# Another order of eight heads, sweeps half a step ahead, and one bfloat16 matmul for a sum, in a bidirectional linear-attention block

## The chip, the cores and the metric

The kernel runs on one core of a Trainium2 chip. The metric is the device time of one execution in microseconds (us); lower is better. Five engines work side by side, each through its own queue in order: TensorE (PE; its weight loads are shown apart, as PEld), VectorE (DVE), ScalarE (ACT), GpSimd (POOL) and SyncE (SP, which issues most transfers).

## What is computed

One transformer block on 2048 tokens of width 1024, with 256 context tokens and a conditioning vector `c`. Cut to what matters:

```python
mod_x = silu(c) @ w_mod + b_mod                    # six vectors: sh1 sc1 g1 sh2 sc2 g2
hx = rmsnorm(x) * (1 + sc1) + sh1                  # and hc from the context, with its own vectors
p = hx @ w_in                                      # queries, keys or gates, values of 8 heads
# heads 0-3, HGRN2: f = lb + (1 - lb) * sigmoid(z), decay f per key element, both directions
# heads 4-7, retention: rope on q and k, one decay per head, both directions
mixed = norm and gate of (forward scan + backward scan)    # scans start from context states
x = x + g1 * (mixed @ w_out)
gate, up = split(rmsnorm2(x) @ w_up); gate = conv3(gate)
x = x + g2 * ((silu(gate) * up) @ w_down)
return rmsnorm(x) * final_g
```

## The kernel before

Every large product is made of float16 pairs: a float32 value is a rounded float16 and a float16 rest, and `mm3` (lines 88 to 90) adds three of the four products. Blocks are combined so that seven block products stand for eight (`unit`), whose inputs, called features (`hx` for the tokens, `hc` for the context), are sums and differences of blocks that `first_blocks` makes once and keeps in DRAM (`hxd`).

The program has these stages. `setup` loads the first slices of `w_mod` and the last 512 tokens. `heads` forms the modulation and the features of the last token group, and then walks 32 steps: eight heads with four token groups (512 tokens) each, the last group first. In step (h, i) `step` runs the backward scan of head h on group 3 - i (`hg_sweep1` for HGRN2, `ret_sweep1` for retention), and the forward scan of the head before it on group i (`hg_sweep2`, `ret_sweep2`), which leaves the scaled output to a second part (`hg_sweep2b`, `ret_sweep2b`: multiply, transpose on PE, store). The projection of the next group or head is a generator that `weave` puts between the pieces of the step. In the first steps of the first head the features of the context and of groups 1 and 0 are still made, also as pieces (`with_blocks`). An HGRN2 scan works through seven levels; at each DVE multiplies the tiles `K` and `Q` by products of gates, and PE multiplies pieces of them into `sc` or `sf`. A retention scan has one product of scores (`rsc`), one multiply with a table (`rA`) and four small state updates. During the heads, `tick` also prepares the next head's weights (`w_z`, `w_q`, `w_vg`: `wx<-raw` rows), and in the retention heads the later slices of the modulation: `mod_later` multiplies rows of `w_mod` into `macc` on DVE. `ret_consts` makes the tables of retention; it is called at the third head.

After the heads come the output product (`opp`), the up product of the feed-forward part (`ffn_up`: 11 pairs of column blocks, with the weights of each of the two halves of a pair prepared one unit ahead in `up_weights`, so 22 times), and the down product (`ffn_down`). `up_weights` squares the raw weights on ACT, sums the squares over partitions on PE (`allsum`), and takes a power of two from the sum on DVE (`pow2`).

The order on each engine is decided at build time by a scheduler that reorders the instructions of the program text; each engine then runs its list in order. The line that sums over partitions before:

```python
self.nc.tensor.matmul(o, self.onesq, cols[:, i:i + 1], start=i == 0, stop=i == n - 1, ...)   # float32, twice
```

Of the kernel before, what the change touches and what calls it, by code (L numbers as in the profile page):

```python
# [43 lines left out]
SEQUENCE = 0, 1, 5, 6, 4, 3, 2  # L44

# [9 lines left out]
class Kern:  # L55
# [57 lines left out]

    def allmax(self, col, tag="tu"):
# [10 lines left out]
    def setup(self):  # L125
# [42 lines left out]
        self.W0, self.items0 = self.head_weights(0)  # L168
# [22 lines left out]
        self.smalls = s2, s1  # L191

# [32 lines left out]
    def mod_rows(self, rows, nr, j4):  # L225
# [12 lines left out]
        bm = view(self.sv, V_BM + 4 * j4, [[1, 4], [0, nr]])  # L238
        nc.vector.tensor_tensor(o, ps[:, :, :nr], bm, ALU.add)

    def mod_loads(self):
# [4 lines left out]
        for j4, places in ((2, ("hx",) * 4), (3, ("hx",) * 4), (0, KEPT[:4]), (1, ("FG", "KTt", "ou0", "ou1"))):  # L246
# [8 lines left out]
            if j4 in (3, 1):  # L255
                self.items0[0 if j4 == 3 else 4][0]()
# [14 lines left out]
    def mod_later(self, j4):  # L271
# [5 lines left out]
        def item(k0):  # L277
            def load():

                st[k0] = w = [self.slot_tile([P, 512], F32, "q", "wm") for _ in range(2)]  # L280
                for kk in range(2):
                    nc.sync.dma_start(w[kk], wsrc[:, k0 + kk, 512 * j4:512 * j4 + 512])

            def comp():
                if k0 == 0:
                    st["acc"] = self.slot_tile([P, 512], F32, "FG", "macc")
# [9 lines left out]
                if k0 + 2 == KT:  # L296
                    self.mod_rows(acc, 1, j4)
# [209 lines left out]
    def unit(self, mm, shape, banks, temps, evac, lin=(None, None), first=False):  # L507
# [5 lines left out]
        if first:  # L513
# [28 lines left out]
            add(tb, tb, u, ALU.add)  # L542
# [123 lines left out]
    def head_weights(self, h):  # L666
# [11 lines left out]
        for nm, tag, cols in want:  # L678
            raws, st = [], {}

            def load(cols=cols, raws=raws, tag="ou2" if h == 0 and nm == "q" else "wr"):
# [4 lines left out]
            def start(nm=nm, tag=tag, raws=raws, st=st):  # L686
# [7 lines left out]
                s, neg, dq = self.scales(self.allsum(ssq), self.dqx[:, 0:1] if h else None, "dq" + nm)  # L694
# [23 lines left out]
    def decay_gates(self, FG, X, h, n, W, first=False):  # L718
# [6 lines left out]
        yield from self.head_unit(*self.fm(w, X, n // 2), evac, first=first)  # L725
# [59 lines left out]
    def hg_proj(self, pool, h, g, W, pr, cur, first=False):  # L785
# [3 lines left out]
        yield from self.decay_gates(FG, X, h, G, W, first)  # L789
# [20 lines left out]
        yield from self.head_unit(*self.tm(w, X, H), evac, (dq, None), first)  # L810
# [125 lines left out]
    def hg_sweep2b(self, pool, h, g, st):  # L936
# [4 lines left out]
        m = r["qf"] if h < NH - 1 else pool.tile([P, G], F32, tag="Kl", bufs=KL, name="m")  # L941
# [3 lines left out]
    def weave(self, main, filler, n_main, n_fill):  # L945

        done = 0
# [8 lines left out]
    def step(self, h, i, W, cur, prev, pr):  # L956
# [3 lines left out]
        slot = i if h % 2 == 0 else NG - 1 - i  # L960
        hg, hgp = h < NH, h - 1 < NH
        if h < 2 * NH:
# [3 lines left out]
        if prev is not None:  # L966
# [880 lines left out]
```

## Time and profile before

| what | value |
|---|---|
| runs | 2703.32 us median of 3 (2699.55 to 2703.4) |
| the profiled execution's own time | 2701.94 us |
| its span, first to last instruction | 2699.5 us |
| busy on PE, DVE, ACT, POOL | 2544.2, 1847.7, 1344.8, 785.0 us |
| mean granted clock of PE | 0.973 of full speed |

Busy time is the union of an engine's instructions; the span less PE's busy time, 155.3 us, is what PE stood idle. A granted clock below 1 in a stretch means that part of it ran at the lower of two levels (1.2 instead of 2.4 GHz).

### The profile page before, as it was taken

The page shows a single profiled execution, that of the slowest core. Times are in us where ns is not written, and L with a number is a line of the kernel's source. Part 1 is how long each engine was busy: PE and PEld are TensorE (multiplying, and loading weights), DVE is VectorE, ACT ScalarE, POOL GpSimd, SP SyncE. Part 2 cuts the span into 40 slices and gives each one's busy share as a digit, 9 for nine tenths or more (in the row PEclk, how much of TensorE's full clock was granted, in tenths as well). Part 3 has the DMA queues.
Part 4 walks back from the last instruction along what each step waited for, and adds up shares of the span by engine and source line. Part 5 has one row for each costly group of instructions (what it writes and reads, how often), then busy time and mean ns, then how long its engine had stood idle before and what let it go on. Part 6 is the DMA issues. An engine that isn't in the chain of part 4 may idle for free.

```text
span 2699.5 us, 56351 instructions
## 1 busy us (share of the span) xinstructions
PE 2544.2 (94%) x22829; PEld 1680.0 (62%) x22829; DVE 1847.7 (68%) x3585; ACT 1344.8 (50%) x2902; POOL 785.0 (29%) x905
## 2 busy tenths in 40 slices
PE   5798999999999999998999999999999999999998
PEld 2578888888889889886454444444444444444443
DVE  4898677776767686666466788888787777323553
ACT  5776456564555444445455566565555555311120
POOL 3733112111223232221344344343443342000102
PEclk7899999999999999998999999999999999999999
DMA  8224234243337575755521232333322325635552
GB/s 297 104 87 158 96 111 146 88 138 119 121 127 257 197 246 178 239 195 180 196 98 47 94 110 101 107 105 110 117 101 103 118 88 197 254 129 187 203 194 95
DMA packets 213621, 393.98 MB, mean 146 GB/s; under 512 B 15599, under 2 KB 97747, under 8 KB 208752
## 3 DMA queue, kind: packets, MB, share of 16 engines
q1 hardware_dynamic: 203808, 373.42, 40.1%
q10 hardware_dynamic: 9248, 16.79, 1.9%
q8 instruction: 178, 2.92, 0.4%
q14 instruction: 83, 0.68, 0.1%
q0 software_dynamic: 304, 0.17, 0.0%
HBM read 298.57 MB, written 91.75 MB: 145 GB/s over the span
## 4 chain that ended last, share of the span: by engine, by line
PE 71%; DVE 15%; ACT 4%; issue 4%; DMA 3%; POOL 2%; SPq 0%; DVEq 0%; ACTq 0%; POOLq 0%
PE pa L88 8%; PE pa L89 8%; PE pa L90 8%; PE pd L89 5%; PE pd L90 5%; PE pd L88 5%; PE pc L88 4%; PE pc L89 4%; PE pc L90 4%; PE pb L88 2%; PE pb L90 2%; PE pb L89 2%; PE opp L89 2%; PE opp L88 2%; PE opp L90 2%
## 5 line engine op out<-in xcount | busy, mean ns | idle before, releaser
L88 PE MATMUL pa<-feat,w 128*128 128x512 f16 x704 | 267.9, 381 | 12.2 <-ACT ta L549 8.1
L89 PE MATMUL pa<-feat,w 128*128 128x512 f16 x704 | 268.1, 381 | 0.0
L90 PE MATMUL pa<-feat,w 128*128 128x512 f16 x704 | 264.9, 381 | 0.0
L89 PE MATMUL pd<-wd,actl 128*128 128x512 f16 x616 | 233.3, 379 | 0.0
L90 PE MATMUL pd<-wd,actl 128*128 128x512 f16 x616 | 233.3, 379 | 0.0
L88 PE MATMUL pd<-wd,actl 128*128 128x512 f16 x616 | 232.7, 379 | 0.0
L89 PEld LDWEIGHTS <-w 128*128 128x128 f16 x1232 | 120.8, 98 | 155.4 <-issue 15.6
L90 PEld LDWEIGHTS <-w 128*128 128x128 f16 x1232 | 121.4, 99 | 145.1 <-issue 1.4
L88 PEld LDWEIGHTS <-w 128*128 128x128 f16 x1232 | 121.7, 99 | 141.6 <-issue 2.4
L89 PEld LDWEIGHTS <-hx 128*128 128x128 f16 x1824 | 183.0, 100 | 8.5 <-issue 6.3
L90 PEld LDWEIGHTS <-hx 128*128 128x128 f16 x1824 | 182.6, 100 | 3.4 <-issue 2.6
L88 PEld LDWEIGHTS <-hx 128*128 128x128 f16 x1824 | 182.9, 100 | 2.2
L1598 DVE SCALAR_TENSOR_TENSOR st<-act,modT,st 128x512 f16<-128x512 f32 x154 | 144.3, 966 | 32.3 <-ACT st L1597 32.3
L1597 ACT ACTIVATE st<-act,modT 128x512 f16<-128x512 f32 x154 | 107.2, 718 | 83.9 <-DVE act L1587 30.2
L88 PE MATMUL pa<-w_vg,hx 128*128 128x128 f16 x800 | 144.7, 222 | 0.2
L89 PE MATMUL pa<-w_vg,hx 128*128 128x128 f16 x800 | 144.5, 222 | 0.0
L90 PE MATMUL pa<-w_vg,hx 128*128 128x128 f16 x800 | 144.4, 222 | 0.0
L88 PE MATMUL pc<-feat,w 128*128 128x512 f16 x352 | 133.5, 379 | 1.3 <-ACT feat L1372 1.2
L88 PE MATMUL pa<-hx,w_z 128*128 128x256 f16 x464 | 127.6, 275 | 7.5 <-DVE rV L591 4.1
L90 PE MATMUL pc<-feat,w 128*128 128x512 f16 x352 | 133.6, 380 | 0.0
L89 PE MATMUL pc<-feat,w 128*128 128x512 f16 x352 | 133.6, 380 | 0.0
L89 PE MATMUL pa<-hx,w_z 128*128 128x256 f16 x464 | 127.3, 274 | 0.0
(551 smaller groups left out, 7557.6 us busy)
## 6 DMA issues: line engine op xcount, KB each, us to landing
hx<-hxd SPq DMA_DIRECT2D x212, 512.0 KB, 4.7
actd<-st SPq DMA_DIRECT2D x154, 256.0 KB, 2.0
actl<-actd SPq DMA_DIRECT2D x28, 1024.0 KB, 5.0
wur<-in_w_up_dram SPq DMA_DIRECT2D x44, 512.0 KB, 3.9
raw<-in_w_in_dram SPq DMA_DIRECT2D x36, 512.0 KB, 4.6
wm<-in_w_mod_dram SPq DMA_DIRECT2D x64, 256.0 KB, 4.1
hxd<-hx SPq DMA_DIRECT2D x28, 512.0 KB, 3.4
wdb<-in_w_down_dram SPq DMA_DIRECT2D x44, 256.0 KB, 3.9
```

What stands on the lines that cost most here:

```text
L88: mm(ps, lhs(0), rhs(0), start=start, stop=False, skip_group_check=True)
L89: mm(ps, lhs(0), rhs(1), start=False, stop=False, skip_group_check=True)
L90: mm(ps, lhs(1), rhs(0), start=False, stop=stop, skip_group_check=True)
L1597: nc.scalar.activation(p[:, 0], v, AF.Copy, scale=s)
L1598: nc.vector.scalar_tensor_tensor(p[:, 1], v, s, p[:, 0], ALU.mult, ALU.subtract)
```

## The change

The heads are taken in the order `ORDER = 4, 0, 1, 2, 3, 5, 6, 7`: the first retention head, the four HGRN2 heads, the other three retention heads. Positions are now called `p`, heads `h`. The features of the context and of groups 1 and 0 are made beside that retention head, with another spacing of pieces in `with_blocks`. `ret_consts` moves to `setup`, with its loads on ACT's queue, and `lower_bounds` from before the first head into its second step.

In `step` the forward scan of the previous head runs half a step ahead: group 0 and, from the middle on, group 1 in step 0, group 2 from the middle of step 1, group 3 from the middle of step 2. Steps of a retention head start with two pieces of the projection (`lead`). `mod_later` makes slices 4 to 9 beside heads 5 and 6 (before: 4 to 11 beside heads 4, 5 and 6); slices 10 and 11, and the broadcast of `g2` from them, move into the first blocks of the down product (`gates_later`). `up_weights` calls `allsum16`: DVE adds the two columns into a bfloat16 one, and PE sums it with one bfloat16 matmul.

```diff
+ORDER = 4, 0, 1, 2, 3, 5, 6, 7
...
+    def allsum16(self, cols, tag):
+        both = self.wp.tile([P, 1], BF16, tag="both", bufs=2, name="both")
+        self.nc.vector.tensor_tensor(both, cols[:, 0:1], cols[:, 1:2], ALU.add)
+        o = self.ps(tag, [P, 1], "allsum")
+        self.nc.tensor.matmul(o, view(self.onesb, 0, [[0, P]]), both, start=True, stop=True, skip_group_check=True)
+        return o
...
-        self.W0, self.items0 = self.head_weights(0)
+        self.ret_loads()
+        self.W0, self.items0 = self.head_weights(ORDER[0], True)
...
+        self.ret_consts()
...
     def with_blocks(self, proj, blocks):
-        for j in range(18):
+        for j in range(14):
             next(proj)
-            if j in (5, 6, 7, 8, 9) or j > 11:
+            if 0 < j < 6 or j > 7:
                 next(blocks, None)
...
-        if prev is not None:
-            (self.hg_sweep2 if hgp else self.ret_sweep2)(pool, (h - 1) % NH, i, prev)
+        if prev is not None and (last or i == 0):
+            sweep2(pool, hp % NH, i, prev)
...
-        if prev is not None:
-            (self.hg_sweep2b if hgp else self.ret_sweep2b)(pool, (h - 1) % NH, i, prev)
+        if prev is not None and (last or i == 0):
+            sweep2b(pool, hp % NH, i, prev, not hg)
+        ahead = prev is not None and not last and i + 1 < NG
+        if ahead:
+            sweep2(pool, hp % NH, i + 1, prev)
         yield from main
...
+        if ahead:
+            sweep2b(pool, hp % NH, i + 1, prev, not hg)
...
-        first = self.hg_proj(pool, 0, NG - 1, W, pr, cur, True)
+        first = self.ret_proj(pool, ORDER[0] % NH, NG - 1, W, pr, cur, True)
...
-                        mods = [it for c in ((4, 5, 6), (7, 8, 9), (10, 11))[h - NH] for it in self.mod_later(c)]
+                        mods = [it for c in ((4, 5, 6), (7, 8, 9))[ORDER[p] - 5] for it in self.mod_later(c)]
...
-            if s == 4 * 2:
-                self.ret_consts()
+                self.lower_bounds()
...
-        s, neg, dq = self.scales(self.allsum(ssq, "sc"), self.dqx[:, 1:2], ("dqz", "dqvg")[ty])
+        s, neg, dq = self.scales(self.allsum16(ssq, "sc"), self.dqx[:, 1:2], ("dqz", "dqvg")[ty])
...
+    def gates_later(self):
+        for j4 in (10, 11):
+            ahead = None
+            for load, comp in self.mod_later(j4, ("wr", "ou0"), True):
+                load()
+                yield
+                if ahead:
+                    ahead()
+                    yield
+                ahead = comp
+            ahead()
+            yield
+        dg = self.slot_tile([P, 2, P], F32, "xs", "diag")
+        self.broadcast_cols(lambda j: dg[:, j % 2], self.gb, 40)
+        yield
...
                 self.work(1)
+                if n < 3:
+                    next(late, None)
```

What the scheduler makes of it is shown at three places. The first is DVE's list in step 1 of the third HGRN2 head, ahead of the first multiply of `Q` (`Q<-Q,FG`, level 1). `KTt` and `Sb` rows are the backward state of the step before; `Sf`, `ou<-ou,o` and `ou<-ou,gate` are the forward scan of the previous head. Before:

```order
L888 SCALAR_TENSOR_TENSOR Sb<-KTt,T_7262,ub 128x128
L102 TENSOR_SCALAR p2i<-p2t 128x1
L907 SCALAR_TENSOR_TENSOR ou<-Sf,T_4400,ou 128x128
L932 TENSOR_TENSOR ou<-ou,o_8044 128x512
L103 TENSOR_SCALAR p2s<-p2i 128x1
L663 TENSOR_TENSOR dq<-p2i,dqx 128x1
L907 SCALAR_TENSOR_TENSOR ou<-ou,T_4400 128x128
L933 TENSOR_TENSOR ou<-ou,gate 128x512
L658 TENSOR_SCALAR neg<-p2s 128x1
L907 SCALAR_TENSOR_TENSOR ou<-ou,T_4400 128x128
L853 TENSOR_TENSOR Q<-Q,FG 128x2x256
```

The same place now, on to the multiply of level 2:

```order
L903 SCALAR_TENSOR_TENSOR Sb<-KTt,T_9050,ub 128x128
L104 TENSOR_SCALAR p2i<-p2t 128x1
L105 TENSOR_SCALAR p2s<-p2i 128x1
L678 TENSOR_TENSOR dq<-p2i,dqx 128x1
L673 TENSOR_SCALAR neg<-p2s 128x1
L868 TENSOR_TENSOR Q<-Q,FG 128x2x256
L870 COPY_PREDICATED Ad<-masks,sc 128x128
L664 SCALAR_TENSOR_TENSOR w_z<-raw,p2s,w_z 128x512
L922 SCALAR_TENSOR_TENSOR Sf<-ou,T_6243 128x128
L664 SCALAR_TENSOR_TENSOR w_z<-raw,p2s,w_z 128x512
L938 TENSOR_TENSOR ou<-ou,o_10025 128x512
```

The rows of the forward scan that stood ahead of level 1 are gone from there, and those of the next group stand between levels 1 and 2, among the preparations of `w_z`.

The second place is the start of DVE's list now, where the tables of retention (`tmp`, `re`, `Dm`) stand behind the first use of the conditioning vector:

```order
L198 TENSOR_TENSOR silb<-silb,p_234 128x8x2
L1117 TENSOR_SCALAR tmp<-tmp 128x8
...
L1128 TENSOR_TENSOR tmp<-tmp 128x8
L1141 TENSOR_TENSOR re<-re,ramp 128x256
L1142 TENSOR_TENSOR Dm<-re 128x128
L1141 TENSOR_TENSOR re<-re,ramp 128x256
L1142 TENSOR_TENSOR Dm<-re 128x128
```

They stood in the third head before, and now come ahead of the copy of the small vectors.

The third place is PE's list in the up product, at the sum of squares (`col` sums per column, `allsum` over all). Before:

```order
L1488 LDWEIGHTS w_27113
L1488 MATMUL col<-onesb,w_27113 128x1
L111 MATMUL allsum<-ssqw,ones 128x1 x2
L90 LDWEIGHTS w_26814
L90 MATMUL pb<-feat,w_26814 128x512
```

And now:

```order
L1525 LDWEIGHTS w_27073
L1525 MATMUL col<-onesb,w_27073 128x1
L121 LDWEIGHTS onesb
L121 MATMUL allsum<-both,onesb 128x1
L90 LDWEIGHTS w_26773
L90 MATMUL pb<-feat,w_26773 128x512
```

Two float32 matmuls became one bfloat16 matmul, between the same neighbours; on DVE a row `both<-ssqw 128x1` stands ahead of it.

## Rows read from the trace of the kernel before

**Rows 1.** Windows; busy us (instructions) of PE, PEld, DVE, ACT, POOL; clock, DMA share, GB/s.

```profile
45.00:105.20 60.20, 38.91 (x335) 31.16 (x335) 54.92 (x105) 47.42 (x113) 42.38 (x48) 0.74 0.37 132
105.20:296.90 191.70, 162.38 (x2502) 142.18 (x2502) 167.87 (x359) 125.77 (x315) 80.36 (x98) 0.91 0.34 121
296.90:463.30 166.40, 158.14 (x2586) 142.81 (x2585) 114.04 (x262) 89.22 (x224) 30.36 (x36) 0.98 0.38 126
463.30:626.50 163.20, 151.64 (x2520) 136.10 (x2519) 120.26 (x283) 100.81 (x253) 29.82 (x36) 0.99 0.36 117
626.50:792.00 165.50, 156.29 (x2562) 140.51 (x2562) 113.43 (x250) 84.91 (x213) 29.74 (x36) 0.98 0.36 120
792.00:908.90 116.90, 110.72 (x1327) 105.35 (x1326) 84.65 (x158) 56.34 (x140) 36.56 (x36) 0.99 0.66 219
908.90:1029.70 120.80, 113.18 (x1373) 107.44 (x1372) 83.76 (x154) 54.82 (x138) 34.95 (x36) 0.99 0.66 220
1580.00:2270.00 690.00, 688.30 (x3473) 320.20 (x3473) 548.78 (x949) 399.19 (x698) 273.00 (x182) 1.00 0.32 108
2270.00:2699.50 429.50, 420.22 (x1955) 191.44 (x1953) 186.47 (x278) 87.58 (x166) 40.24 (x120) 0.99 0.49 183
```

**Rows 2.** Tile `sd`, first score product of an HGRN2 step: ns, first and last start.

```profile
L823 PE MATMUL sd<-qs,ks x512: 196/196/263, 105.2 to 756.1; 128*32 128x32 f32 x171
```

**Rows 3.** Windows of step 0 of the second, third and fourth HGRN2 head.

```profile
296.90:354.80 57.90, 57.90 (x875) 52.62 (x874) 32.56 (x91) 26.28 (x68) 3.29 (x7) 1.00 0.31 103
463.30:519.30 56.00, 51.08 (x801) 46.21 (x800) 37.68 (x110) 36.43 (x96) 3.81 (x7) 1.00 0.23 73
626.50:680.20 53.70, 53.70 (x816) 48.60 (x815) 31.79 (x90) 23.17 (x62) 3.29 (x7) 1.00 0.23 78
```

**Rows 4.** Timeline of ACT at the start and in the third head [idle before, releaser].

```profile
15.54 0.63 ACT L368 ACTIVATE junk<-hc 128x512 f16<-128x512 f32 x1 [10.93 <-DMA hc<-in_x_dram]
...
463.61 1.28 ACT L1079 ACT_TABLE_LOAD   x1
...
480.07 0.68 ACT L1102 ACTIVATE re<-ramp,tmp 128x128 f32<-128x128 f32 x2
```

**Rows 5.** Tile `macc` (ns min/median/max), and eight feature transposes on PE's timeline.

```profile
L295 DVE SCALAR_TENSOR_TENSOR macc<-wm,silc,macc x56: 733/744/2722, 819.6 to 1099.2; 128x512 f32<-128x512 f32 x56
...
146.65 1.04 PE L386 MATMUL tp<-ident,x 128*128 128x128 f32 x8
```

**Rows 6.** Waits of PE over the whole run: us in total, times, longest.

```profile
PE sc L837 <- DVE Q L853: 13.9, 4, 3.7
...
PE sf L844 <- DVE Q L853: 10.9, 5, 4.7
```

**Rows 7.** Timeline of DVE in step 1 of the third HGRN2 head: start, us.

```profile
524.93 0.68 DVE L932 TENSOR_TENSOR ou<-ou,o 128x512 f32<-128x512 f32 x1
...
525.66 0.34 DVE L907 SCALAR_TENSOR_TENSOR ou<-ou,T 128x128 f32<-128x128 f32 x1
...
537.03 1.75 DVE L649 SCALAR_TENSOR_TENSOR w_z<-raw,p2s,w_z 128x512 f16<-128x512 f32 x1
...
539.31 1.78 DVE L853 TENSOR_TENSOR Q<-Q,T 128x512 f32<-128x512 f32 x1
```

**Rows 8.** PE's timeline at a sum in the up product, and the weight loads of `col`.

```profile
1657.56 0.47 PE L1488 MATMUL col<-onesb,w 128*128 128x1 bf16 x13
1657.89 0.58 PE L111 MATMUL allsum<-ssqw,ones 128*128 128x1 f32 x4
1658.34 0.38 PE L90 MATMUL pb<-feat,w 128*128 128x512 f16 x1
...
L1488 PEld LDWEIGHTS <-w x320: 95/96/98, 1516.6 to 2228.5; 128*128 128x128 bf16 x160
```

**Rows 9.** Timelines of ACT and DVE just ahead of that sum.

```profile
1656.25 0.19 ACT L1483 ACTIVATION_READ_ACCUMULATOR w<-wur 128x1 f32 x1
...
1657.65 0.75 DVE L1567 SCALAR_TENSOR_TENSOR act<-ta,taps,act 128x511 f32<-128x511 f32 x1 [1.94 <-ACT act L1562]
```

More of the change, by code (lines that the diff above doesn't have):

```diff
@@ L278, in load @@
             def load():
-                st[k0] = w = [self.slot_tile([P, 512], F32, "q", "wm") for _ in range(2)]
+                if places[0] == "wr":
+                    wr = self.slot_tile([P, 2, 512], F32, "wr", "wm")
+                    st[k0] = w = [wr[:, i] for i in range(2)]
+                else:
+                    st[k0] = w = [self.slot_tile([P, 512], F32, places[0], "wm") for _ in range(2)]
                 for kk in range(2):
@@ L541, in unit @@
             evac(1, 0, t4, None)
-            add(tb, tb, u, ALU.add)
+            self.last = add(tb, tb, u, ALU.add)
             evac(1, 1, tb, None)
@@ L679, in head_weights, with load @@
             raws, st = [], {}
-            def load(cols=cols, raws=raws, tag="ou2" if h == 0 and nm == "q" else "wr"):
+            def load(cols=cols, raws=raws, tag="wr"):
                 for c in cols:
@@ L693, in start @@
                                          accum_out=ssq[:, i:i + 1])
-                s, neg, dq = self.scales(self.allsum(ssq), self.dqx[:, 0:1] if h else None, "dq" + nm)
+                s, neg, dq = self.scales(self.allsum(ssq), None if first else self.dqx[:, 0:1], "dq" + nm)
                 W[nm] = w, dq
@@ L788, in hg_proj @@
         FG = self.slot_tile([P, 2, G], F32, "FG", "FG")
-        yield from self.decay_gates(FG, X, h, G, W, first)
+        yield from self.decay_gates(FG, X, h, G, W)
         qs = pool.tile([P, G], F32, tag="qs", bufs=1, name="qs")
@@ L940, in hg_sweep2b, with weave @@
         tp = self.head_transpose(r["op"])
-        m = r["qf"] if h < NH - 1 else pool.tile([P, G], F32, tag="Kl", bufs=KL, name="m")
+        m = pool.tile([P, G], F32, tag="Kl", bufs=KL, name="m") if own else r["qf"]
         nc.scalar.copy(m, tp.rearrange("p c t -> p (c t)"))
         nc.scalar.dma_start(self.mixd[h][:, g * G:(g + 1) * G], m)
-    def weave(self, main, filler, n_main, n_fill):
-        done = 0
+    def weave(self, main, filler, n_main, n_fill, lead=0):
+        done = lead
+        for _ in range(lead):
+            next(filler)
         for j, _ in enumerate(main):
@@ L954, in weave, with step @@
             pass
-    def step(self, h, i, W, cur, prev, pr):
+    def step(self, p, i, W, cur, prev, pr):
         pool = self.mp
         g = NG - 1 - i
-        slot = i if h % 2 == 0 else NG - 1 - i
-        hg, hgp = h < NH, h - 1 < NH
-        if h < 2 * NH:
+        slot = i if p % 2 == 0 else NG - 1 - i
+        last = p == 2 * NH
+        h = None if last else ORDER[p]
+        hg = not last and h < NH
+        hp = ORDER[p - 1]
+        hgp = hp < NH
+        if not last:
             main = (self.hg_sweep1 if hg else self.ret_sweep1)(pool, h % NH, g, slot, pr, cur)
@@ L1162, in ret_proj @@
         for i, r in enumerate((cos, sin)):
[L1163 removed]
+            (nc.sync if first else nc.scalar).dma_start(r, self.I["rope"][:, i, g * G:(g + 1) * G])
         w, dq = W["z"]
```

102 lines of the change are left out of this document (54 added, 48 removed).

## The prediction

> **What bounds the kernel now.** The page's first part comes first: PE is busy for 2544.2 of 2699.5 us, so at most 155.3 us can be won without taking work from PE. The windows then say where PE stands idle. In the up product PE is busy 688.3 of 690.0 us at full clock [rows 1]: there only PE's own work counts. Before the first head's scores begin (105.2 us, [rows 2]) and in the first head it is different. From 45.0 to 105.2 us PE is busy all the time by its rows, but at a clock of 0.74, which is a mean of the two levels; DVE is busy for 54.92 of these 60.2 us. The first head takes 191.7 us; PE is busy 162.38, at a clock of 0.91, while DVE is busy 167.87, a share of 0.876. The other HGRN2 heads take 163.2 to 166.4 us with DVE at 113 to 120, the first two retention heads 116.9 and 120.8 with DVE at 84. So the first head is bound by DVE, and the rest by PE with small gaps. Whose gaps they are, the waits say: in the HGRN2 heads the longest are PE's for DVE's `Q`, 13.9 us in 4 waits and 10.9 us in 5 [rows 6].
>
> **The start and the first head.** The same features and the same eight heads have to be made; what changes is beside which head the features of the context and of groups 1 and 0 are made. I put together what a retention head with features would take, once from DVE's side and once from PE's.
>
> DVE: the two retention heads need 84.65 and 83.76 us, mean 84.2 [rows 1]. In them are 24 `macc` products for the modulation each, which are not made in the new first head: 24 x 0.744 = 17.9 the median of its row [rows 5]. That leaves 66.3. What the features take on DVE is the difference of the first HGRN2 head to the three others: 167.87 - (114.04 + 120.26 + 113.43)/3 = 52.0. Sum 118.3; at the share that DVE reached in the old first head, 0.876, this takes 135.
>
> PE: a retention head takes (116.9 + 120.8)/2 = 118.9. To that come the features' transposes, which in the trace are groups of eight of 1.04 us [rows 5]; there are ten such groups, 10.4 us. Sum 129, if PE hides everything else.
>
> I take 133, between the two and nearer to DVE's, as DVE was the fuller engine in the old first head. The bounds are 129, and the whole surplus of the old first head over the others put on a retention head: 191.7 - (166.4 + 163.2 + 165.5)/3 = 26.7, so 118.9 + 26.7 = 145.6.
>
> The tables of retention leave the third head. In step 0 of that head PE is idle for 56.00 - 51.08 = 4.9 us, in the same step of the heads around it for 0.0 [rows 3]; in that step ACT loads a table and works on `re` [rows 4]. I count those 4.9 us as won, so an HGRN2 head takes (166.4 + 163.2 - 4.9 + 165.5)/3 = 163.4. At the old place ACT's part of the tables lasts from the load at 463.61 to `re` at 480.07 + 0.68, 17.1 us with other work between [rows 4]. In `setup` ACT waits there for 10.93 us for the context [rows 4], and DVE is not yet loaded; but new loads of the tables' inputs stand on ACT's queue ahead of it. I count +1.5 us at the start, with bounds of 0 (all of it in the idle time) and 17.1 - 10.9 = 6.2 (what the idle time does not hold).
>
> End of the first five heads: 105.2 + 1.5 + 133 + 4 x 163.4 = 893.3, where four HGRN2 heads and one retention head end at 908.9 now [rows 1]. That is **-15.6 us**, with 129 instead of 133 it is -19.6, and with 145.6 it is -3.0.
>
> **The sums of squares.** In the up product the two float32 matmuls with their weight loads begin at 1657.89 and the next product at 1658.34: 0.45 us that PE spends on a sum [rows 8]. A bfloat16 matmul of the same form is `col`: 13 of them take from 1657.56 to 1657.89, 0.025 us each. 22 sums x (0.45 - 0.025) = **-9.3 us**. The weight load of such a matmul takes 96 ns by its rows [rows 8], but lies beside matmuls. The Trainium skill ("TensorE: Matmul & The Clock Gate", section "LDWEIGHTS (loading the stationary operand)") states that a load takes its columns divided by 1.2 in ns, 107 for 128; the row says 96. Were it exposed, a sum would cost 0.132 and the term would be 22 x (0.45 - 0.132) = -7.0; as 13 pairs in a row take 0.33 us together, I go by the row and let loads overlap.
>
> What the term costs on DVE is `both`, one add of 128x1, 22 times. No wait of PE results if it is early. ACT's sum of squares is read at 1656.25 + 0.19, 1.45 us before PE comes to it, and DVE has been idle for 1.94 us just before 1657.65 [rows 9]. But a product of 0.75 us can stand ahead of `both`, so in some of the 22 PE may wait a little. From below the term is 0: `both` makes PE wait 0.43 us each time.
>
> **Half-step sweeps.** In step 1 of an HGRN2 head six instructions of the previous head's forward scan stand ahead of the first `Q` now, four of 0.34 and two of 0.68 us [rows 7], 2.7 us; in the changed list they have gone from there and stand between levels 1 and 2. PE's longest waits for `Q` are at the third level of step 1, and by then DVE has, in the changed list, as much to do as before: the sweep's rows moved, they did not vanish. In step 2 fewer rows stand ahead, in step 0 more. So I count a small part of 13.9 + 10.9 = 24.8 us [rows 6]: **-4 us**. Bounds: -14, if the first kind of wait (`sc`) goes away; and +8, if the moved rows make PE wait 0.5 us in each of 16 HGRN2 steps. What is late if the moved rows take their place badly: the `Q` of level 2, behind it K and Q of later levels, and on PE the `sc` and `sf` products with everything that follows, since PE's list is in order.
>
> **The late gates.** Slices 10 and 11 of the modulation bring 16 products on DVE into the down product: 16 x 0.744 = 11.9 us [rows 5], and 16 small matmuls on PE that were made anyway. From 2270.0 to the end DVE is busy for 186.47 of 429.5 us [rows 1], so this cover is ample: **0**. In the third retention head 16 products fewer stand on DVE, but PE is the bound there. If the cover failed (as when PE has to take the sum before its product is there), it would cost up to 11.9. `lower_bounds` and `lead` move little: 0, with no bound beyond those of the half-step.
>
> **Sum.** -15.6 - 9.3 - 4 + 0 = -28.9 us on the profiled execution's own 2701.94 us (span 2699.5 and 2.4 around it), which gives 2673.0. The median of the runs is 1.4 us above that execution: **2674 us**.
>
> **Rivals.**
>
> *A, the start does not pay.* The features' work takes as long beside a retention head as beside an HGRN2 head. For it: the features wait for the same loads and for a chain through ACT, PE and DVE; ACT was busy 125.77 us in the first head [rows 1], more than the 116.9 us that a retention head takes. Against it: ACT's own part for a retention head is smaller too (56.34 against 84.91 to 100.81). Price: first head 145.6, term -3.0, sum -3.0 - 9.3 - 4 = -16.3: 2687.
>
> *B, the half-step pays fully.* PE no longer waits in `sc` for `Q`: -14 instead of -4, so 2664. For it: 2.7 us of DVE's work leave the place before the first `Q`, and the longest of these waits is 3.7 us [rows 6]. Against it: the third level's tally.
>
> *C, slower.* The sweep's rows, put into the middle of a step, delay `Q` and `K`, and PE waits in every one of 16 HGRN2 steps. Speaking for it: DVE is busy 113 to 120 of some 165 us in these heads, the middle of a step has `w_z` at 1.75 us and `Q` at 1.78 us [rows 7], and one more instruction of that length ahead of a `Q` that PE already waits for is paid in full. The point from which it decides is (15.6 + 9.3)/16 = 1.56 us a step; at 2.5 us a step it costs 40: 2703.4 - 24.9 + 40 = 2718. Against it: the work is the same in sum, and in the steps 2 and 3 less of it is left.
>
> *D, `both` makes PE wait.* DVE's queue in the up product is 548.78 of 690.0 us full [rows 1]; if `both` comes 0.43 us late each time, the sums bring nothing: 2674 + 9.3 = 2683.
>
> **How the numbers follow.** Forecast (all terms near what I took, 2664 to 2682): 0.54. A: 0.2. B: 0.08. D: 0.05. C: 0.07. Another 0.06 goes to two of the cases A, D and a part of C together, which leaves the time within 0.2% of before. 0.2% of 2703.3 is 5.4 us, about what a measurement of this kernel can tell from no change. Faster by more than that: 0.54 + 0.2 + 0.08 + 0.05 = 0.87; the same 0.06; slower 0.07. The range goes below to B with the first head at 129 (2664 - 4 = 2660) and 3 us for the start's cost and the third head's tables; above to A with half-step sweeps that cost something (2687 + 4 + 5 = 2696). So 2657 to 2696; C and the case of no change lie outside.
>
> **What would show it.** In the changed trace the first `rsc` product, with which the first head's scores begin, should start near 106.7 us; the first HGRN2 head's first `sd` should start 133 us later, near 240; the last HGRN2 head should end near 893. In step 0 of the heads PE should nowhere be idle for 5 us because of tables. A sum in the up product should take 0.03 us on PE from the last `col` to the next `pb`, up to 0.13 if the load shows; a wait of `allsum` for `both` of more than 0.1 us speaks for D. Waits of `sc` and `sf` for `Q` should fall from 24.8 to about 21 us; under 12 is B, and waits for `Q` or `K` in every step are C. The down product should stay at 429.5 us, with DVE at about 198. The prediction is wrong if the features, and not the head, set the length of the first head (A), if the first scores start later than 110 us, or if new waits in the HGRN2 steps add up to more than 20 us.

## The result and the profile after

The changed kernel takes 2710.65 us (median of 7 runs, 2705.7 to 2713.18), the kernel before 2699.55 on the same occasions (7 runs): ratio 1.0038, 95% interval 1.0027 to 1.0049. It is 10 us slower, where I forecast 29 us less. (A thousandth of the ratio is 2.7 us; the differences below are worked out in this way from the ratios.) The profiled run spans 2708.9 us, before 2699.5.

The first scores of the first head, now `rsc`, and the first `sd` of an HGRN2 head (tile views; ns min/median/max, first and last start):

```profile
L838 PE MATMUL sd<-qs,ks x512: 196/196/263, 272.2 to 880.0; 128*32 128x32 f32 x171
...
L1243 PE MATMUL rsc<-K x128: 275/275/557, 110.6 to 1230.3; 128*128 128x128 f32 x128
```

The windows that answer to those of [rows 1]: the end of the start, the first head, the four HGRN2 heads, two retention heads, and the up product (columns as there).

```profile
45.00:110.60 65.60, 40.45 (x325) 32.12 (x325) 61.57 (x106) 48.13 (x118) 46.82 (x56) 0.71 0.34 122
110.60:272.20 161.60, 129.61 (x1340) 115.85 (x1340) 124.20 (x229) 100.47 (x247) 74.68 (x90) 0.88 0.42 149
272.20:430.70 158.50, 151.18 (x2553) 136.45 (x2552) 111.60 (x262) 86.67 (x219) 31.11 (x36) 0.99 0.38 126
430.70:590.20 159.50, 152.01 (x2532) 137.08 (x2531) 113.99 (x263) 86.63 (x218) 29.00 (x36) 0.99 0.37 119
590.20:750.90 160.70, 154.29 (x2524) 139.03 (x2523) 114.28 (x263) 86.80 (x220) 29.11 (x36) 0.98 0.36 119
750.90:914.90 164.00, 156.42 (x2582) 141.10 (x2582) 110.26 (x250) 85.71 (x217) 31.52 (x36) 0.99 0.38 125
914.90:1034.40 119.50, 110.09 (x1333) 104.78 (x1331) 87.91 (x163) 56.41 (x139) 37.42 (x36) 1.00 0.66 219
1034.40:1149.90 115.50, 108.53 (x1292) 102.53 (x1290) 79.26 (x159) 48.82 (x125) 28.48 (x32) 0.99 0.67 222
1580.00:2270.00 690.00, 686.37 (x3435) 314.38 (x3434) 560.60 (x976) 401.28 (x705) 279.24 (x185) 1.00 0.32 110
```

The first scores start at 110.6 (forecast 106.7). The first head takes 161.6 us (forecast 133), the HGRN2 heads 160.7 on the mean (forecast 163.4), and the first five heads end at 914.9 (forecast 893.3; before 908.9). From there the last three heads and the rest up to the first `opp` product take 356.3 us, before 352.9. The loss of the whole kernel is already there at the first `opp`: 1271.2 us, before 1261.8.

The first head, cut into its steps 0 and 1, in which the features are made, and its steps 2 and 3. Before:

```profile
105.20:219.80 114.60, 92.78 (x1348) 80.11 (x1348) 106.30 (x228) 81.01 (x216) 62.92 (x85) 0.88 0.28 105
219.80:296.90 77.10, 69.61 (x1156) 62.07 (x1155) 61.57 (x132) 44.76 (x101) 17.44 (x13) 0.95 0.44 143
```

and after:

```profile
110.60:221.90 111.30, 83.58 (x818) 72.65 (x819) 85.73 (x160) 69.19 (x185) 59.06 (x80) 0.85 0.39 145
221.90:272.20 50.30, 46.02 (x524) 43.20 (x522) 38.48 (x70) 31.27 (x63) 15.62 (x10) 0.97 0.48 159
```

This is the main reading. The two steps with features take 111.3 us now and 114.6 before, though PE has 818 instead of 1348 matmuls there and DVE 85.73 instead of 106.30 us of work. PE's idle time is 27.7 us now (111.30 - 83.58) and 21.8 before, and the clock is about as low (0.85 and 0.88). So DVE's total, 77% of the time, does not set the length of these steps now. Before, DVE was busy for 93% of them, so there it may have; that the two lengths are nearly equal does not by itself show one cause. PE's longest waits in the changed first head:

```profile
PE pa L90 <- DVE ct L545: 5.0, 1, 5.0
PE pb L91 <- DVE hc L419: 3.5, 4, 2.0
PE rob L1263 <- DVE Kt L1265: 3.4, 2, 2.1
PE pa L91 <- DVE hc L419: 3.4, 1, 3.4
PE pa L90 <- DVE ftmp L432: 3.2, 1, 3.2
```

`hc` holds features of the context, `ftmp` is a step on the way to features, `ct` is a partial sum of the projection, and `Kt` is retention's own state. In the whole head the waits for `hc`, `ftmp` and the normed rows `x`, from which features are made, add up to 15 us of the 32 that PE is idle.

The sums of squares, in PE's timeline at one of the 22 places, answering to [rows 8]:

```profile
1668.93 0.49 PE L1525 MATMUL col<-onesb,w 128*128 128x1 bf16 x14
1669.29 0.16 PE L121 MATMUL allsum<-both,onesb 128*128 128x1 bf16 x1
1669.31 0.38 PE L90 MATMUL pb<-feat,w 128*128 128x512 f16 x1
```

The next product starts 0.02 us after the sum, where it was 0.45. Over all sums of the up product these distances add up to 0.81 us, before to 10.25: 9.4 us less, and my term was 9.3. But from the first to the last column sum the stretch is 818.4 us now and 825.3 before, 6.9 less.

Two of PE's longest waits over the whole run, answering to [rows 6] (the longest, 13.1 us for `hx`, was 13.3 before):

```profile
PE rob L1263 <- DVE Kt L1265: 11.2, 7, 2.4
PE sc L852 <- DVE Q L868: 10.4, 6, 3.2
```

`Q` is waited for less: 11.5 us with the 1.1 of `sf`, before 24.8. But 10.2 of those 24.8 us stood in the old first head, which is an HGRN2 head without a forward scan beside it; the changed first head is of retention and has no `Q` to wait for. Only the rest can be the half-step's. `rob`, the use of retention's backward state, is new near the top; it was 3.0 us.

### The profile page after: what moved, and what is told of

It reads as the page before. It is cut to its first block, busy times and chain, and to the rows that moved or that the text cites. A ratio compares the mean times of both kernels' runs of the same rounds, so it can differ in the third digit from the quotient of the medians.

```text
span 2708.9 us, 56234 instructions
## 1 busy us (share of the span) xinstructions
PE 2543.7 (94%) x22763; PEld 1671.7 (62%) x22763; DVE 1859.2 (69%) x3608; ACT 1340.2 (49%) x2908; POOL 781.1 (29%) x905
## 4 chain that ended last, share of the span: by engine, by line
PE 68%; DVE 16%; DMA 6%; issue 4%; ACT 3%; POOL 2%; SPq 0%; DVEq 0%; POOLq 0%; ACTq 0%
PE pa L90 8%; PE pa L92 8%; PE pa L91 8%; PE pd L91 5%; PE pd L92 5%; PE pd L90 5%; PE pc L90 4%; PE pc L92 4%; PE pc L91 3%; PE pb L90 2%; PE pb L91 2%; PE pb L92 2%; DMA raw<-in_w_in_dram 1%; PE opp L92 1%; PE opp L91 1%
## 5 line engine op out<-in xcount | busy, mean ns | idle before, releaser
L91 PEld LDWEIGHTS <-hx 128*128 128x128 f16 x1824 | 182.4, 100 | 12.4 <-issue 10.4
L91 PE MATMUL pa<-w_vg,hx 128*128 128x128 f16 x800 | 145.6, 223 | 0.0
L90 PE MATMUL pa<-hx,w_z 128*128 128x256 f16 x464 | 127.8, 275 | 15.2 <-DVE rV L606 6.2
L91 PEld LDWEIGHTS <-w_z 128*128 128x128 f16 x1072 | 108.2, 101 | 36.4 <-issue 25.0
```

The lines of the kernel that those rows point to most:

```text
L90: mm(ps, lhs(0), rhs(0), start=start, stop=False, skip_group_check=True)
L91: mm(ps, lhs(0), rhs(1), start=False, stop=False, skip_group_check=True)
```

## The experiments

The theory after this reading: the features cost PE about the same time beside either kind of head, so the new order has no gain in the first head (T1). Rivals: the half-step sweeps cost what the order gains (T2, my rival C), or the late gates or the sums do (T3).

**The parts alone, on the kernel before.**

e1, the sum alone:

```diff
-        s, neg, dq = self.scales(self.allsum(ssq, "sc"), ...)
+        s, neg, dq = self.scales(self.allsum16(ssq, "sc"), ...)
```

> The kernel before with the bfloat16 sum alone. In the trace of the changed kernel the stretch from the first to the last column sum of the up product takes 818.4 us, before 825.3. If the sums give this, the kernel is 7 us faster (my term was 9.3); if the add on VectorE makes TensorE wait (rival D), it is within 2 us of before, and the 6.9 us come from something else.

Measured 2696.35 us, ratio 0.9986 (0.9976 to 0.9997): 3.8 us faster (0.8 to 6.5), which is less than the 7 expected; the interval ends just short of it. The stretch of the up product in its trace, and DVE's longest wait in it:

```profile
1398.80:2222.20 823.40, 803.97 (x4049) 371.59 (x4048) 652.18 (x1114) 473.55 (x840) 337.59 (x259) 0.99 0.29 99
```
```profile
DVE both L117 <- ACT w L1491: 41.4, 12, 4.6
```

PE is busy 7.3 us less than before (811.3), but idle for 19.4 us instead of 14.0. No wait of PE is for `both`; it waits more for ACT's squares (3.4 us, once) and for weights (3.2 us, once). This trace is the slowest of its kind. From the first to the last column sum the nine traces of this case with the old sums take 824.7 to 829.3 us (mean 826.6), the eight with the new ones 817.1 to 823.4 (mean 819.7): 6.9 us less, with PE 7.8 us less busy and 1.0 us more idle on the mean.

e1 also shows how far one trace can be trusted. Up to the first `opp` product its lists on PE, DVE, ACT and POOL are those of the kernel before, instruction by instruction; yet it comes there 5.1 us earlier. From the first score to the first `opp`, before and e1:

```profile
105.20:1261.80 1156.60, 1066.49 (x15433) 978.60 (x15434) 842.30 (x1839) 623.90 (x1563) 294.46 (x349) 0.97 0.47 157
105.40:1256.70 1151.30, 1061.47 (x15433) 974.56 (x15434) 841.39 (x1839) 624.25 (x1563) 295.66 (x349) 0.97 0.47 158
```

PE's idle time is the same, 90.1 and 89.8 us; its busy time differs by 5.0. In e12, e13 and e14 below, which are also alike up to there, the idle time is 83.9, 84.4 and 87.2 us and the busy time 1060.4 to 1063.4. So between two single traces, some 5 us of busy time and 3 us of idle time over the heads can differ without any change in the program.

e2, the gates alone: `mod_later` for heads 4 and 5 only, and `gates_later` in the down product.

```diff
-                    if NH <= h < 2 * NH - 1:
-                        mods = [... ((4, 5, 6), (7, 8, 9), (10, 11))[h - NH] ...]
+                    if h in (NH, NH + 1):
+                        mods = [... ((4, 5, 6), (7, 8, 9))[h - NH] ...]
```

> The kernel before with slices 10 and 11 of the modulation moved into the down product, nothing else. My prediction put this at 0. If the moved slices are the reason that the changed kernel's way from the last column sum to the end is 5.5 us longer (64.3 + 412.1 against 60.8 + 410.1), the kernel is 4 to 6 us slower than before, less what the third retention head wins without them (0 to 2 us). If those 5.5 us have another reason, it is within 1 us.

Measured 2704.03, ratio 1.001 (0.9998 to 1.0022): 2.7 us slower, and no change is not excluded. What stands near zero is a sum of two larger terms. The third retention head takes 104.5 us in e2 and in e11 below, both without the slices, and 110.8 to 112.6 in the traces of the old order that have them and no half-step beside retention: 6 to 8 us gained. From the last column sum to the end, the five traces with late gates take 476.4 to 478.2 us and the twelve others 470.7 to 471.4: some 5.5 us lost, in e2 itself 7. (In the trace of e2 the first `opp` starts at 1252.1 instead of 1261.8, but about 5 of these 9.7 us are within what e1 shows without any change there.)

e3, the half-step sweeps with the leading pieces, in the old order, and e6, the same without the leading pieces. The edit of e3 is that of the change in `step` and `weave`; in e6 `weave` gets no `lead`.

> The kernel before with the half-step sweeps and the two leading pieces in retention's steps, in the old order of heads. Forecast: 4 us faster. If rival C is the cause of the loss, the heads get longer and the kernel is 10 us slower or more. If the order of heads is the cause, this one is between 8 us faster and 4 us slower.

> The kernel before with half-step sweeps everywhere, but no two leading pieces of the projection in retention's steps. If the leading pieces cause the 14.6 us that the retention heads lost, this kernel is within 4 us of before or faster; if the sweeps' place does, it is 9 us slower or more.

Measured e3 2716.15, ratio 1.0057 (1.0044 to 1.007), 15 us slower; e6 2716.46, ratio 1.0051 (1.0038 to 1.0065), 14 us slower. The leading pieces are not the cause. The window over the four retention heads in e3:

```profile
788.90:1228.10 439.20, 409.14 (x4843) 387.18 (x4842) 298.79 (x584) 195.72 (x493) 117.63 (x125) 0.98 0.62 206
```

and before:

```profile
792.00:1216.60 424.60, 402.68 (x4817) 382.56 (x4816) 295.71 (x580) 194.54 (x488) 118.23 (x125) 0.99 0.64 212
```

PE's waits in these windows, first in e3, then before:

```profile
PE pa L88 <- DVE rV L591: 11.0, 3, 4.8
PE rob L1236 <- DVE Kt L1238: 9.7, 7, 2.4
```
```profile
PE pa L88 <- DVE rV L591: 4.1, 2, 2.1
...
PE rob L1227 <- DVE Kt L1229: 3.0, 5, 1.2
```

The loss is in the retention heads, 14.6 us. T2 holds for the half-step alone, but at another place than rival C put it: what is late is not `Q` in HGRN2 steps but the small state updates `Kt` and the combination `rV` in retention steps. That they are late because the forward scan of the next group stands ahead of them is read from the lists; e15 below tests it.

e5, half-step sweeps only where the step's own head is HGRN2:

```diff
-        if prev is not None and (last or i == 0):
+        if prev is not None and (not hg or i == 0):
...
-        ahead = prev is not None and not last and i + 1 < NG
+        ahead = prev is not None and hg and i + 1 < NG
```

> The kernel before with half-step sweeps only in steps of HGRN2 heads; steps of retention heads as before, without leading pieces. In the run with the half-step everywhere the three HGRN2 heads that have a head ahead of them took 493.1 us (before 495.0) and the retention heads 439.2 (before 424.6). If the loss is in the retention heads alone, this kernel is 1 to 5 us faster than before; if the sweeps cost in HGRN2 heads too, it is slower than before.

Measured 2700.33, ratio 0.9995 (0.9986 to 1.0004): 1.4 us faster, not told from no change, nor from the forecast 4. Its waits for `Q` are 21.2 us instead of 24.8: 3.6 less, as I had forecast for the half-step. So beside HGRN2 the wait shrinks as expected, and the gain in time is little or nothing.

e8, the tables of retention in `setup`, with `ret_loads` ahead of the first weights and `ret_consts` behind the small vectors:

```diff
-            if s == 4 * 2:
-                self.ret_consts()
...
+        self.ret_loads()
         self.W0, self.items0 = self.head_weights(0)
...
         self.smalls = s2, s1
+        self.ret_consts()
```

> The kernel before with retention's tables made in the setup, loads on ScalarE's queue, nothing else. My forecast for this part alone: 1.5 us at the start, 4.9 won in the third head, so 3.4 us faster. If the tables are what makes the changed kernel's first scores 5.4 us late, the first head starts at 109 to 111 us and the kernel is within 1.5 us of before.

Measured 2695.65, ratio 0.9982 (0.9974 to 0.9991): 4.9 us faster. The first scores start at 107.5, 2.3 later; over the traces in the old order it is 106.0 to 107.7 in five with the tables in `setup` and 104.9 to 105.7 in the others. Step 0 of the third head has no idle time any more.

**The order.** e4 is the changed kernel without the sums, the half-step, the leading pieces and the late gates; slices 4 to 11 stand beside heads 5 and 6, four each.

> The changed kernel without the bfloat16 sums, without the half-step sweeps and leading pieces, and with slices 10 and 11 of the modulation beside retention heads again (four slices beside each of heads 5 and 6): what is left is the order of heads, the features beside the retention head and the tables in the setup. If the order is the cause of the loss, the first scores start near 110 us again and the kernel is 8 to 16 us slower than before. If it gains as I forecast and the half-step loses it, the kernel is 12 to 18 us faster.

Measured 2734.05, ratio 1.013 (1.0113 to 1.0146), 35 us slower. This says that the order does not gain, but not how much it costs: its heads 5 and 6 take 127.0 and 127.2 us with four slices each, which neither kernel has. The first head took 160.2 us. Both halves of the expectation missed.

A cleaner pair differs in the order and what comes with it: the head beside which features are made, the spacing of the pieces in `with_blocks`, the place of `lower_bounds` and of a few first loads. e7 is the changed kernel with half-step sweeps only beside HGRN2 heads and no leading pieces (the edit of e5 in its `step`). e11 is the kernel before with the sums, the tables in `setup`, the late gates and the edit of e5.

> The changed kernel with half-step sweeps only in steps of HGRN2 heads, and no leading pieces. If half-step sweeps beside retention heads are the loss, the three retention heads at the end get 8 to 12 us shorter, and the kernel is within 4 us of before, where the changed one is 11 slower. If the order of heads alone is the loss, it stays 8 to 12 us slower.

> Everything of the change but the order of heads, with half-step sweeps only beside HGRN2 heads: bfloat16 sums, tables in the setup, late gates. The parts alone gave -3.8, -4.9, +2.7 and -1.4 us by their ratios, together -7. The same set with the new order was 6 us slower than before. If the order is what costs, this one is 5 to 9 us faster than before, so the order costs 11 to 15; if the parts work against each other, it is within 2 us of before.

Measured e7 2708.14, ratio 1.0022 (1.0013 to 1.003); e11 2693.72, ratio 0.9964 (0.9951 to 0.9977). The order costs 0.0058, 16 us, with intervals of 2 to 4 us on either. The half-step beside retention, with its leading pieces, costs 4 us in the new order (1.0038 against 1.0022, intervals that just overlap), less than in the old one. That the order does not gain, as T1 says, is shown; T3 falls.

Where the order's time goes, in windows of the two: the first head, the HGRN2 heads without features, the rest of the heads up to the first `opp`, and all of these. e11:

```profile
106.20:299.10 192.90, 161.80 (x2494) 140.73 (x2494) 166.73 (x357) 126.81 (x318) 79.04 (x96) 0.91 0.35 119
299.10:787.70 488.60, 465.30 (x7665) 418.61 (x7665) 338.94 (x777) 261.47 (x655) 90.31 (x108) 0.99 0.37 122
787.70:1250.70 463.00, 434.06 (x5255) 414.08 (x5254) 318.60 (x668) 222.73 (x560) 120.90 (x143) 0.98 0.62 204
106.20:1250.70 1144.50, 1061.15 (x15410) 973.42 (x15410) 824.27 (x1801) 611.01 (x1532) 290.25 (x347) 0.97 0.47 155
```

e7:

```profile
111.60:274.30 162.70, 129.82 (x1339) 116.20 (x1339) 123.64 (x229) 100.60 (x247) 75.51 (x91) 0.85 0.42 148
274.30:915.10 640.80, 611.33 (x10186) 550.87 (x10186) 450.17 (x1038) 345.81 (x870) 120.83 (x144) 0.99 0.38 123
915.10:1268.30 353.20, 326.38 (x3907) 310.02 (x3907) 246.88 (x539) 167.42 (x422) 88.35 (x107) 0.98 0.64 210
111.60:1268.30 1156.70, 1067.54 (x15429) 977.09 (x15430) 820.69 (x1805) 613.83 (x1537) 284.69 (x342) 0.97 0.46 153
```

PE is idle in the first head for 31.1 us in e11 and 32.9 in e7: the same beside either head. An HGRN2 head without features leaves 23.3 / 3 = 7.8 and 29.5 / 4 = 7.4 us: the same too, but there is one more of them outside the cover. The rest of the heads has 28.9 and 26.8. So PE is idle 5.8 us more, and busy 6.4 us more for nearly the same number of matmuls. With the start's 5.4 us that makes the 17.6 by which e7 comes later to the first `opp`. Of these terms the start is clear of the spread (traces of the same instructions start within 1.6 us), the idle time is more than the 3.3 us seen without a change, and the busy time is little more than the 5.0 between before and e1. It goes with the clock: in the first head it is 0.85 instead of 0.91, which is 2 x 0.15 x 162.7 = 49 us at the lower level instead of 35. In the changed kernel's own trace it is 0.88, 39 us.

e9 and e10 leave out the features of groups 1 and 0 in the kernel before and in the changed one:

```diff
-                blocks = self.first_blocks(1, rows(1, ...), ...)
...
-                blocks = self.first_blocks(0, rows(0, ...), ...)
...
-            self.nc.sync.dma_start(X[m], self.hxd[g][m])
+            self.nc.sync.dma_start(X[m], self.hxd[max(g, 2)][m])
```

> The kernel before without the features of groups 1 and 0 (those of group 2 are read in their place, so the output is another). In the first head these features are made in steps 0 and 1, which take 114.6 us; a step 0 and 1 of the later HGRN2 heads takes 93 to 98. If the features set the length of these steps, the kernel gets 15 to 27 us faster here and clearly more in the changed kernel. If features cost the same beside either head, both kernels get faster by the same 20 to 30 us.

> The changed kernel with the same left out: the features of groups 1 and 0, with those of group 2 read in their place. Its steps 0 and 1 take 111.4 us, nearly as long as those of an HGRN2 head with features, though a later retention head needs 57 to 66 for these two. If the features set the length, the first head (161.7 us) gets 35 to 50 us shorter; if they cost the same beside either head, 20 to 30; by my forecast (133 against 118.9) it would be 14.

Measured e9 2670.11, ratio 0.9884 (0.9864 to 0.9903), 31 us faster than before; e10 2678.66, ratio 0.9909 (0.9891 to 0.9928), 35 us faster than the changed kernel. The first heads, e9 and then e10:

```profile
105.60:276.60 171.00, 154.63 (x2501) 138.49 (x2500) 128.14 (x293) 93.42 (x230) 37.64 (x42) 0.94 0.37 127
```
```profile
109.80:234.60 124.80, 109.90 (x1266) 103.15 (x1264) 78.03 (x151) 62.58 (x145) 39.40 (x42) 0.92 0.53 175
```

The features of groups 1 and 0 cost the whole kernel the same 31 to 35 us in both orders, within the intervals. In the first head itself it is 20.7 us beside HGRN2 and 36.8 beside retention; beside HGRN2 the next head's step 0 also gets 8.3 us shorter without them (57.9 to 49.6). The rival in the expectation, the same price beside either head, holds for the kernel; the larger price for the retention head holds in the first head only. The edit takes a little more away than the features: with no feature pieces to mix in, the projections of the first two steps also use the kernel's ordinary order of block products.

Steps 0 and 1 of the first head, e9 and then e10, to be read against 114.60 and 111.30 with features:

```profile
105.60:198.20 92.60, 84.46 (x1366) 75.37 (x1365) 67.79 (x163) 48.23 (x134) 22.06 (x32) 0.94 0.39 137
109.80:182.70 72.90, 62.81 (x730) 58.83 (x729) 41.18 (x85) 33.44 (x88) 26.69 (x34) 0.88 0.57 195
```

In the new order the two steps are 38.4 us shorter without these features: PE is busy 20.8 us less and idle 17.6 us less.

Without these features the changed kernel is still behind (0.9909 against 0.9884: 7 us, an interval of 7 either way). It holds all the other parts too, which by e11 and the pair of the changed kernel and e7 bring 0.0036 - 0.0016 = 0.0020. So the order by itself costs about 0.0045 there, 12 us, with an interval of some 9 either way, and 16 with the features: as far as these runs tell, most of its cost does not come from making these features beside another head.

**A better version, and what the sums lose.** e12 is e1, e5 and e8 together, in the old order.

> The kernel before with bfloat16 sums, tables in the setup and half-step sweeps beside HGRN2 heads only; old order, old place of the gates. Sum of the parts: -3.8 - 4.9 - 1.4 = -10 us. If the parts add up, it is 7 to 12 us faster than before and the best of all; if they share the same gaps, 4 to 6.

Measured 2690.91, ratio 0.9954 (0.994 to 0.9969): 12 us faster than before. The parts add up within the interval. e11 is e12 with the late gates, and is 0.0010 slower, as in e2.

e13 and e14 put the add of e12 on ScalarE and on GpSimd:

```diff
-        self.nc.vector.tensor_tensor(both, cols[:, 0:1], cols[:, 1:2], ALU.add)
+        self.nc.scalar.activation(both, cols[:, 0:1], AF.Identity, bias=cols[:, 1:2])      # e13
+        self.nc.gpsimd.tensor_tensor(both, cols[:, 0:1], cols[:, 1:2], ALU.add)            # e14
```

> The best kernel so far (bfloat16 sums, tables in the setup, half-step beside HGRN2 heads only), with the add of the two columns on ScalarE, right behind its own squares, in place of VectorE. If VectorE, which waits 41 us for the squares with this add at the head of its queue, delays TensorE by that, it is 2 to 5 us faster than the same kernel with the add on VectorE (2691); if VectorE had that time to spare, within 1.5 us of it.

> The same with the add on GpSimd. If VectorE's wait is what costs, this too is faster than with the add on VectorE by 2 to 5 us; if GpSimd's queue is in turn held up by the wait, it loses it again and is within 1.5 us of it or slower.

Measured e13 2689.08, ratio 0.9952 (0.9937 to 0.9968); e14 2686.83, ratio 0.9947 (0.9932 to 0.9963). Neither is told from e12, and with intervals of 4 us on each a gain of 2 to 5 is not excluded by the times alone. The traces show none where it would have to be: the stretch of the up product takes 821.1 us in e13 and 818.8 in e14, and 819.1 in e12. On ACT the add waits for nothing. So the theory that DVE's blocked queue takes the rest of the gain is not borne out.

e15 is e6 with the forward scan of the next group behind retention's own step instead of in its middle:

```diff
+        if ahead and hg:
             sweep2(pool, (h - 1) % NH, i + 1, prev)
         yield from main
+        if ahead and not hg:
+            sweep2(pool, (h - 1) % NH, i + 1, prev)
```

> The kernel before with half-step sweeps; beside retention heads the forward scan of the next group stands at the end of the step, behind the step's own state updates, not in its middle. With it in the middle the kernel was 14 us slower than before (with or without the leading pieces), and TensorE waited 9.7 us for the state updates (before 3.0). If the place in the middle is what costs, this is within 4 us of before; if being early costs in any place, it is 9 us slower or more.

Measured 2709.41, ratio 1.0027 (1.0016 to 1.0038): 7 us slower than before, between the two expectations. The place in the middle is about half of the cost (14 less 7, with intervals of 3 to 4 us on either); the other half stays with the sweep at the end of the step. PE's wait of `rob` for `Kt` is even longer, 14.8 us in 8 times, while that of `pa` for `rV` has gone down to 4.8.

## Why the prediction was wrong

**The step that failed** is the length of the first head, "I take 133, between the two and nearer to DVE's". It takes 161.6. That is 28.6 us more; the start is 3.9 later than forecast and the HGRN2 heads are 10.9 shorter, which together are the 21.6 by which the first five heads end later. DVE's work was nearly right (124.2 us, worked out 118.3). Wrong was to divide it by the old first head's share of 0.876, as if that had been DVE's limit over the head. The share was 93% in the two steps with features and 80% in the others (106.30 of 114.60, 61.57 of 77.10), and in the new head it is 77% in both. Wrong in the sum for PE was to add 10.4 us for the transposes and nothing for waits: with the features of groups 1 and 0 PE is busy 20.8 us longer and idle 17.6 us longer in the two steps in which they are made. PE is idle for about 30 us in the first head of either order. Without these features it is 16.4 us beside HGRN2 and 14.9 beside retention (e9, e10), so about half of that idle time is theirs, and the time at the lower clock falls from about 35 and 39 us to 20. The other half remains with the features of the context still there; no run takes those out. Which step of the chain from rows to features sets the pace is not shown either.

**The order's sign.** The first head leaves PE idle for 29 to 33 us whichever head stands there (before, changed, e7, e11), so what counts is how much idle time that head has where it stands without features. An HGRN2 head has 7 to 8 us; the retention head that the old order has in addition, without slices of the modulation, has 1.1:

```profile
1024.40:1128.90 104.50, 103.39 (x1272) 99.15 (x1271) 69.47 (x139) 48.47 (x123) 25.74 (x32) 1.00 0.58 194
```

(third retention head of e11). The new order has one more of the former and one less of the latter: 6 us by these rows, 5.8 measured. My surplus of 26.7 us was a difference to heads that have such idle time themselves. This is why rival A, "the start does not pay", was right in kind and too small in size: it put the first head at 145.6, and it takes 161.6. By e7 and e11 the order costs 16 us, where my terms without the tables make a gain of 15.6 - 3.4 = 12.2. These 28 us are most of the 39 between forecast and result. In the two traces 5 us of the loss are the start and 6 the idle time; the rest is busy time at the lower clock, which is not told from the spread of single traces. That the head moved brings its idle time with it is read from these sums, not tested by a run of its own.

**The start.** Forecast +1.5 for the tables, measured +2.3 (e8). The rest of the 5.4 us comes with the order: in e7 and e11, which both have the tables, it is 111.6 against 106.2, and the four traces in the new order start at 109.8 to 111.6. I also misread the row of the start: from 45.0 to 105.2 us PE is not "busy all the time" but 38.91 of 60.20 us, so 21.3 us of the 155.3 that PE is idle stand there, and I gave them no term. In the changed kernel's last 6 us before the first score DVE's list has two multiplies of retention's rotated keys, 1.69 and 1.53 us, among the features' rows; that they are the cause was not tested.

**The tables.** Forecast 3.4 us faster, measured 4.9 (2.4 to 7.0), with the idle time of step 0 gone: right.

**The sums.** At the sums themselves the term was right, 9.4 for 9.3. The Trainium skill ("TensorE: Matmul & The Clock Gate", section "LDWEIGHTS (loading the stationary operand)") gives the length of a load as its columns divided by 1.2 in ns, 107 for 128; the rows here have 95 to 98. That a load of this length stands in the way, which would make the term 7.0, was an estimate of mine worked out from that figure, and the skill's section does not say so. The trace does not bear the estimate out: from the product before to the sum, and from the sum to the next product, it is 0.02 to 0.03 us each, at 21 of 22 sums. The stretch of the up product gets 6.9 us of the 9.4, on the mean of all traces, and the end of e1 3.8 (0.8 to 6.5). Rival D named the wrong wait: PE does not wait for `both`. What takes the other 2 to 3 us stays open.

**The half-step.** Forecast -4. Beside HGRN2 it is -1.4 (-3.8 to +1.1, e5). The wait for `Q` shrinks by 3.6 us there, which is the size that I took; but step 0 of the three HGRN2 heads with its two sweeps gets longer, 59.7, 63.7 and 56.6 us instead of 57.9, 56.0 and 53.7. I had taken the whole 24.8 us for the half-step's, though 10.2 of them stood in the first head, which has no sweep to move. Beside retention it costs, 4 us in the new order and 15 in the old (e6 less e5). My sum has no term for it: I looked at the HGRN2 heads alone, where DVE's work is larger. Rival C had the kind of mechanism, the sweep's rows in front of what PE needs next, but for the wrong heads.

**The late gates.** Forecast 0, measured 2.7 with an interval that holds 0. That this is near is luck, as both halves were mis-sized: the third retention head gains 6 to 8 us, which I put at 0 because "PE is the bound there", and the end loses about as much, 5.5 to 7, though DVE was idle for more than half of it.

Together: the sums, tables, half-step beside HGRN2 and gates bring 10 us (e11), the order costs 16 and the half-step beside retention 4: 10 slower, as measured. (This closes by construction, since the last two are differences of the ratios of e7 to its neighbours.)

## What to carry to other kernels

Work that must be ready by a fixed time can have a price of its own in the waits of the bounding engine. Before moving it under another stage, cut the stage at its deadline and compare idle time there, not busy sums over the whole stage. Here the stage with the deadline was idle for as long beside either kind of head, so the head with more idle time of its own elsewhere was the better one to put there. A part has to be measured in the surroundings that it will have: the half-step was worth -1 us beside one kind of head and +15 beside the other. And before reading a difference off two single traces, find two traces of the same instructions and see how far they differ: here up to 5 us in busy time and 3 in idle time.

## What the hardware showed

A bfloat16 matmul of 128x1 with its weight load costs PE 0.025 us between neighbours though its load lasts 0.096 [rows 8]. At one place of e13 it stands alone between products of 512 columns, and there the next product starts 0.03 us behind it. The add of two 128x1 columns took 0.16 to 0.28 us on DVE (medians of the traces; 0.22 in e12), 0.30 on ACT in e13 and 0.20 on POOL in e14, and the choice made no measurable difference to the kernel. PE was at its lower clock for about 35 of 193 us in the first head of e11, and in the first heads of the new order for 39 of 162 (the changed kernel) and 49 of 163 (e7), with nearly the same idle time. The same instructions took 5 us less of PE's busy time in one execution (e1) than in another (before), up to the first `opp`.
